# Where the two operands of a matmul lie in on-chip memory: stationary parts moved to a fixed distance from the moving ones, and the feed-forward's high parts put ahead of its low ones

## The chip, the cores and the metric

The kernel runs on one core of a Trainium2 chip. The metric is device time in microseconds (us) of one launch, the median over runs. TensorE (PE in the profile) multiplies; VectorE (DVE), ScalarE (ACT) and GpSimd (POOL) work on tiles in on-chip memory; SyncE (SP) issues most of the transfers from the chip's main memory.

## What is computed

One layer of a decoder on 256 tokens of 1,024 features, float32 throughout:

```python
h = rms_norm(x);  x = x + hybrid_mixer(h)          # conv module and sparse attention, one projection
h = rms_norm(x);  x = x + cross_attention(h, mem)  # 4 heads of 256, 256 memory tokens
h = rms_norm(x);  x = x + swiglu(h)                # D_FF = 2816
return rms_norm(x, final_norm_g)

def swiglu(h, w_in, w_out):
    a, b = jnp.split(h @ w_in, 2, axis=-1)
    return (jax.nn.silu(a) * b) @ w_out
```

`hybrid_mixer` projects `h` to conv inputs, queries, keys, values and gates; runs a causal 31-tap convolution with a layer norm, and attention over compressed, selected and window keys; gates both, and projects once more.

## The kernel before

**Products in three passes.** A float32 product is made of matmuls of the type fp32r. Each operand is split into a high part, a rounded copy made on ACT (line 179 for weights, 290 for activations), and a low part, the difference, made on DVE (lines 181 and 291). A product is then high × high, high × low and low × high, added up in PSUM. Some projections (`whole`, line 267: k0, kc, vc, q) use plain float32 matmuls without a split.

**The gemms.** The activations are held transposed, feature by token, as tiles of 8 × 256 elements in each of the 128 partitions. A weight block `name` is 1,024 × 256, loaded in two halves of 512 × 256 (`raw`, line 205), each split into two tiles (`split`, line 172). `gemm` (line 257) runs both halves through `rows` (line 235): three passes of 2 × 4 matmuls, 24 per half and 48 per block, each with a stationary operand of 128 × 128 (`lhsT`, loaded by a separate instruction that PE overlaps with the matmul before) and a moving operand (`rhs`) of 128 × 256. Mostly the weights are stationary and the activations move; for vs, vw and v (`nat=True`) the activations are stationary and the weights move.

**Where the tiles lie.** Tiles are given out by tag in the order in which the code first asks for them. The long tiles of 8,192 bytes per partition (tags `L0` to `L14`) and the double one `LL` of 16,384 come first and begin at byte 4,608 = 9 × 512, so all of them lie at 0 modulo 512, and so does every slice of 128 or 256 elements of them. The activations' parts lie in them. Then come five buffers `wh` and five `wl` for the high and low parts of weights. Each is 1,048 elements, 4,192 bytes, so from one buffer to the next the start moves by 96 modulo 512; `at` (line 173) shifts each group of five splits by another 16 bytes. High and low part of one half have the same offset (the buffers of `wl` begin at 480, and the low part 32 bytes into them). So the halves of u0 to u7 lie at 400, 304, 112, 208, 32, 416, 320, 128, 224, 48, 432, 336, 144, 240, 64 and 448; v0's first half at 448; xq1's second half at 64; f8's first half and f20's second at 0; f7's first half at 288. The transposed query tiles of cross-attention (tag `vt`) lie at 0 or 256.

**The order around the change.** Instructions run on each engine in the order that the scheduler gives them from the code; `behind(...)` holds an instruction until a marked one has been issued before it on the same engine, and `in_line()` does that for PE's own sequence. In the attention part (lines 813 to 880) the 8 head pairs go one after the other: `scores` for the next pair (PE, then DVE with line 735 for the first 128 tokens and 741 for the others), `weights` (ACT's exp, line 756), some rows of gc and v gemms from `between`, then `turned` (PE transposes, line 777, and ACT copies, line 780, listed in `copies`). The softmax over compressed blocks, `compressed_weights` (lines 692 to 704), is one set of instructions on the tile `nsc`; it is called in the first period ahead of that period's `weights`, and its result is transposed at line 857 in the third. `first[...]` names instructions behind which a given split is held. The convolution's taps run on POOL (lines 424 and 428), ACT (426) and DVE (412) beside the gemms of the first 180 us.

**The feed-forward** (lines 1046 to 1065) loops over 22 blocks j of `ffn_in_w`, each with 128 columns of a (b = 0) and 128 of b (b = 1). The moving operand of the high pass is `fg[:, :, kb]`, high and low part of the activations side by side, 512 columns; the low pass moves 256. Per j the order is: b = 0 high (8 matmuls), b = 0 low (8), b = 1 high, b = 1 low. Even j use the PSUM banks of `mm`, odd j those of `s`, two each. The result u is split into three pairs of long tiles. At the end (lines 1075 to 1083) u's parts are stationary and the weights `fo` move, 512 columns, 264 matmuls.

Of the kernel before, what the change touches and what calls it, by code (L numbers as in the profile page):

```python
# [15 lines left out]
P = 128  # L16
# [82 lines left out]
def tile_hybrid_block(  # L99
# [26 lines left out]
    def longs(names, slots, dt=F32R):  # L126
        return [long(n, i, dt=dt) for n, i in zip(names, slots)]

    def twin(name, dt=F32R):

        t = sb.tile([P, 2, NB, S], dt, tag="LL", name=name)
        return t, t[:, 0], t[:, 1]

    def small(name, shape, dt=F32, tag=None, bufs=1):
# [26 lines left out]
    def roots(at):  # L161

        return nc.scalar.activation(table[:, at:at + 1], eps_t[:, 0:1], AF.Sqrt)
# [6 lines left out]


    def split(w, shape, name):
        at = 4 * (len(splits) // 5 % 5)
        hi, lo = (small(f"{name}{c}", [P, 1024 + 24], F32R, tag=f"w{c}", bufs=5)[:, n:n + 1024].rearrange("p (k c) -> p k c", k=shape[1])
                  for c, n in (("h", at), ("l", at + 8)))

        n = 2 if name == "k1_0" else shape[1]
        with behind(*first.get(name, ())):
            copies = [nc.scalar.activation(hi[:, at:at + n], w[:, at:at + n], AF.Copy) for at in range(0, shape[1], n)]  # L179
            for at in range(0, shape[1], n):  # L180
                low = nc.vector.tensor_tensor(out=lo[:, at:at + n], in0=w[:, at:at + n], in1=f(hi[:, at:at + n]), op=ALU.subtract)  # L181
        splits[name] = copies[-1], low
        return hi, lo
# [13 lines left out]
    def ahead(name, slot, pieces=(4, 4)):  # L197
# [3 lines left out]
        for n in pieces:  # L201
            nc.sync.dma_start(w[:, at:at + n], wst[CHUNK_AT[name]][:, at:at + n])
            at += n

    def raw(name, i):

        if name in held:
            return held[name][:, 4 * i:4 * i + 4]
        w = small(f"{name}_{i}", [P, 4, 256], tag="w", bufs=4)
        loads[f"{name}_{i}"] = nc.sync.dma_start(w, wst[CHUNK_AT[name]][:, 4 * i:4 * i + 4])  # L210
        return w

# [146 lines left out]
    for name, slot in (("k2", 12), ("k3", 11), ("u0", 13)):  # L359
        ahead(name, slot)  # L360
    roots(0)

    def kx(j):
        ps = gemm(f"k{j}", mem) if j else whole("k0", mem_t)
# [327 lines left out]
    def compressed_weights(*marks):  # L692

        mc = small("mc", [P, 2, HEADS])
        with behind(*marks):
            nc.vector.tensor_reduce(out=mc, in_=nsc, axis=AX.X, op=ALU.min)
        with behind(*marks, mins_of[1]):
            nc.vector.tensor_tensor(out=nsc, in0=nsc, in1=mc.unsqueeze(3).to_broadcast([P, 2, HEADS, 16]), op=ALU.subtract)
            nc.scalar.activation(nsc, nsc, AF.Exp, scale=-1.0)
            nc.vector.tensor_reduce(out=sumc, in_=nsc, axis=AX.X, op=ALU.add)  # L700
            nc.vector.scalar_tensor_tensor(out=sumc, in0=sumc, scalar=1e-30, in1=igc, op0=ALU.max, op1=ALU.mult)
            nc.vector.reciprocal(sumc, sumc)
            nc.vector.tensor_tensor(out=sumc, in0=sumc, in1=cpt[:, CP_CM:CP_CM + 2].unsqueeze(2).to_broadcast([P, 2, HEADS]), op=ALU.mult)
            nc.vector.tensor_tensor(out=nsc, in0=nsc, in1=sumc.unsqueeze(3).to_broadcast([P, 2, HEADS, 16]), op=ALU.mult)
# [5 lines left out]
    def scores(hp):  # L710

        g = hp // 2
        nbp = bias_of(hp)
        s0 = aux(f"s0_{hp}", [P, 2, 2, P], "s0", 1)
        p0 = small(f"p0_{hp}", [P, 2, 2, P], tag="p0", bufs=2)
        s1s, p1 = [], []

        def later_half(hd):
            s1 = aux(f"s1_{hd}", [P, 2, S], "s", 2)
            with in_line():  # L720
                for i, t in enumerate((kdh, kdl)):
                    mm = nc.tensor.matmul(s1, lhsT=qh(hd, 1), rhs=t[:, g].rearrange("p b t -> p (b t)"), start=i == 0, stop=i == 1)
            last[:] = [mm]
            s1s.append(s1)

        later_half(2 * hp)
        for k, hd in enumerate(heads_of(hp)):
            with in_line():
                for i, t in enumerate((kdh, kdl)):
                    mm = nc.tensor.matmul(s0[:, k], lhsT=qh(hd, 0), rhs=t[:, g, :, 0:P], start=i == 0, stop=i == 1)  # L730
        last[:] = [mm]
        later_half(2 * hp + 1)
        for k, hd in enumerate(heads_of(hp)):
            for br in range(2):
                red = nc.vector.tensor_tensor_reduce(out=p0[:, k, br], in0=s0[:, k, br], in1=nbp[:, k, P:S], scale=1.0, scalar=3e38,  # L735
                                                     op0=ALU.add, op1=ALU.min, accum_out=mins[:, hd, 0, br:br + 1])
        for k, hd in enumerate(heads_of(hp)):
            p1.append(small(f"p1_{hd}", [P, 2, S], tag="pr", bufs=4))
            for br in range(2):
                with behind(red):  # L740
                    low = nc.vector.tensor_tensor_reduce(out=p1[k][:, br], in0=s1s[k][:, br], in1=nbp[:, k], scale=1.0, scalar=3e38,
                                                   op0=ALU.add, op1=ALU.min, accum_out=mins[:, hd, 1, br:br + 1])
        mins_of.append(low)
        if hp == 1:
            first["gc2_1"] = first["gc3_0"] = red,
        return p0, p1

    def weights(hp, p0, p1, *late):
# [96 lines left out]
    for hp, n in enumerate(PERIODS):  # L845
        if hp < 7:
            p.append(scores(hp + 1))
            if hp == 0:
                compressed_weights(*exp[-2:])
            with behind(*copies[-3:]):  # L850
                weights(hp + 1, *p[hp + 1])
        if hp == 2:
            pc_ps = aux("pc_ps", [P, 4, P], "pt", 2)
            with in_line():
                for qb in range(2):
                    for i in range(2):
                        mm = nc.tensor.transpose(pc_ps[:, 2 * i + qb], nsc[:, qb, 8 * i:8 * i + 8].rearrange("p h n -> p (h n)"), ident)
            last[:] = [mm]
            nc.scalar.activation(pct.rearrange("p i q -> p (i q)"), pc_ps.rearrange("p i q -> p (i q)"), AF.Copy)

        with behind(*last):
            if hp == 3:
                total = rnorm(total, "l")
            elif hp == 5:
                layer_norm_scale(total)
        rest(n - AFTER)
        if len(turns) == 2:
            output(hp // 2 - 1, turns)
            turns = []
        p0, p1 = p[hp]  # L870
        tb = turned(f"b{hp}", [p1[k][:, br, P:S] for k in range(2) for br in range(2)])
        ta = [turned(f"a{hd}", [q for br in range(2) for q in (p0[:, k, br], p1[k][:, br, 0:P])])
              for k, hd in enumerate(heads_of(hp))]
        turns.append((ta, tb))
        if hp == 1:
            with behind(*last, *copies[-3:]):
                total = layer_norm_squares(total)
        rest(AFTER)
# [36 lines left out]
    def residual(products, xin, gain, name, slots):  # L915

        xo = long(f"x_{name}", slots[0])
        g, gh, gl = twin(f"g_{name}") if len(slots) == 1 else (None, *longs((f"gh_{name}", f"gl_{name}"), slots[1:]))
        acc = small(f"acc_{name}", [P, S], tag="vw", bufs=4)
        for j, (n, ps) in enumerate(products):  # L920
            js = slice(2 * j, 2 * j + 2)
# [25 lines left out]

    def cross_queries(j):
        ps = gemm(f"xq{j}", xg)
        queries[j] = [small(f"xq{c}{j}", [P, 2, S], F32R, tag="vt", bufs=4) for c in "hl"]  # L950
        part(queries[j][0][:], queries[j][1][:], ps[:])

    def cross_scores(j):
# [75 lines left out]

    rf = small("rf", [P, S], tag="vw", bufs=4)  # L1030
    nc.scalar.activation(rf, spread(rnorm(acc2, "3"), "3"), AF.Copy)
    uh, ul = (longs([f"u{c}{i}" for i in range(3)], ss) for c, ss in (("h", (4, 2, 1)), ("l", (5, 3, 6))))
    def residual_first():

        banks = [[aux(f"fo{c}_{tb}", [P, 512], t, n) for tb, (t, n) in enumerate(ts)]
# [10 lines left out]
    for j in range(NF):  # L1046
        hs = chunk(f"f{j}")
        ab = small(f"ab{j}", [P, 2, S], tag="pr", bufs=4)
        for b in range(2):

            ps = bank(f"ps_f{j}_{b}") if j % 2 == 0 else aux(f"ps_f{j}_{b}", [P, 2, S], "s", 2)
            cs = slice(b * P, b * P + P)
            for kb in range(NB):
                nc.tensor.matmul(ps, lhsT=hs[kb // 4][0][:, kb % 4, cs], rhs=fg[:, :, kb], start=kb == 0, stop=False)  # L1054
            for kb in range(NB):
                nc.tensor.matmul(ps[:, 1], lhsT=hs[kb // 4][1][:, kb % 4, cs], rhs=fg[:, 0, kb], start=False, stop=kb == NB - 1)  # L1056
            nc.scalar.activation(ab[:, b], ps[:, 0], AF.Copy)  # L1057
            nc.vector.tensor_tensor(out=ab[:, b], in0=ps[:, 1], in1=ab[:, b], op=ALU.add)  # L1058
        nc.vector.tensor_tensor(out=ab, in0=ab, in1=rf.unsqueeze(1).to_broadcast([P, 2, S]), op=ALU.mult)
        sl = small(f"sl{j}", [P, S], tag="sg", bufs=3)  # L1060
        silu = nc.scalar.activation(sl, ab[:, 0], AF.Silu)  # L1061
        nc.vector.tensor_tensor(out=sl, in0=sl, in1=ab[:, 1], op=ALU.mult)
        part(uh[j // 8][:, j % 8], ul[j // 8][:, j % 8], sl[:])
        if j == 2:
            accs = residual_first()

# [8 lines left out]
    def to_output(c, tb, his, los):  # L1075

        ts = slice(tb * P, tb * P + P)
        for k0, hi in his.items():
            for k in range(2):
                kb = k0 + k  # L1080
                th, tl = (u[kb // 8][:, kb % 8, ts] for u in (uh, ul))
                for t, w in ((th, hi), (th, los[k0]), (tl, hi)):
                    nc.tensor.matmul(accs[c][tb], lhsT=t, rhs=w[:, k], start=False, stop=kb == NF - 1 and t is tl)  # L1083

# [158 lines left out]
```

## Time and profile before

| | |
|---|---|
| median of 3 runs | 561.68 us (561.3 to 562.07) |
| the profiled execution | 562.13 us |
| its span, first to last instruction | 560.3 us |
| mean granted clock of PE | 0.997 |
| PE busy | 551.0 us |
| PE's weight loads busy | 508.0 us |
| DVE, ACT, POOL busy | 415.4, 362.5, 146.3 us |
| read from main memory | 95.39 MB |

PE's matmuls overlap: one lasts about 280 ns at 256 columns, but the next starts well before it ends. So the rate is read from starts, not from durations. A row of the view of instructions in order of time has the start, the time that the row's instructions cover, the engine, the line, the operation, what it writes and reads, and the count; a row of the chain has start, time, and what. L246 is line 246 of the kernel.

### The profile page before, as it was taken

The numbers are of one execution on the slowest core, as the hardware profiler recorded it, in microseconds if no ns is written. First come the engines' busy times: TensorE is split into PE (matmuls) and PEld (weight loads), VectorE is DVE, ScalarE is ACT, GpSimd is POOL, SyncE is SP. The second block draws the span as 40 slices with busy tenths as digits, with TensorE's granted clock in tenths as the row PEclk, the third lists the DMA queues.
The fourth block names the chain that finished last, engine by engine and source line by source line (L and its number), as shares of the span: only waits on it lengthen the run. The fifth ranks groups of instructions, "written<-read, shape, count | busy, mean of one in ns | idle before, by whom it ended". The sixth has DMA issues, their size and how long they took to land.

```text
span 560.3 us, 10256 instructions
## 1 busy us (share of the span) xinstructions
PE 551.0 (98%) x3886; PEld 508.0 (91%) x3886; DVE 415.4 (74%) x772; ACT 362.5 (65%) x689; POOL 146.3 (26%) x129
## 2 busy tenths in 40 slices
PE   8999999999999999999999999999999999999995
PEld 7999998889999999999999999988888888888883
DVE  2798985898978999794768666578878787864531
ACT  3577757689957898789546565567565656563421
POOL 0005997989999102000003100230000000000000
PEclk9999999999999999999999999999999999999998
DMA  8938714356365554334554542446555555666601
GB/s 297 412 108 307 301 45 121 113 187 217 128 204 171 180 187 138 99 113 151 176 192 160 185 156 76 150 151 225 181 196 183 192 181 196 183 198 189 189 32 75
DMA packets 29298, 97.31 MB, mean 174 GB/s; under 512 B 3136, under 2 KB 5952, under 8 KB 28992
## 3 DMA queue, kind: packets, MB, share of 16 engines
q1 hardware_dynamic: 28528, 95.34, 51.4%
q10 hardware_dynamic: 720, 1.31, 0.7%
q8 instruction: 30, 0.49, 0.4%
q14 instruction: 20, 0.16, 0.1%
HBM read 95.39 MB, written 1.25 MB: 172 GB/s over the span
## 4 chain that ended last, share of the span: by engine, by line
PE 82%; POOL 7%; ACT 3%; DVE 2%; DMA 2%; issue 2%; ACTq 0%; POOLq 0%
PE ps_f L1054 15%; PE fo L1083 11%; PE ps_u L246 8%; PE ps_f L1056 7%; POOL yt L428 6%; PE ps_pw L246 4%; PE ps_v L246 4%; PE ps_wo L246 4%; PE ps_xq L246 4%; PE ps_k L246 3%; PE ps_q L276 3%; PE ps_xo L246 3%; PE ps_gc L246 2%; DMA mem_t<-in_memt_dram 2%; PE ps_xo L1021 2%
## 5 line engine op out<-in xcount | busy, mean ns | idle before, releaser
L428 POOL TENSOR_TENSOR yt<-yt,vw 128x512 f32<-128x512 f32 x65 | 100.9, 1553 | 56.5 <-ACT vw L426 52.7
L426 ACT ACTIVATE vw<-vt,ppt 128x256 f32<-128x256 f32 x110 | 48.0, 499 | 14.8 <-POOL yt L428 14.6
L1054 PE MATMUL ps_f<-g,f_1h 128*128 128x512 f32 x176 | 48.6, 396 | 0.0
L1054 PE MATMUL ps_f<-g,f_0h 128*128 128x512 f32 x176 | 48.2, 396 | 0.0
L1125 POOL TENSOR_SCALAR x<-x,rr 128x512 f32<-128x512 f32 x1 | 0.7, 693 | 179.8 <-DVE rr L1095 179.8
L181 DVE TENSOR_TENSOR f_1l<-f,f_1h 128x1024 fp32r<-128x1024 f32 x22 | 26.9, 1224 | 22.5 <-ACT sl L1061 18.3
L412 DVE SCALAR_TENSOR_TENSOR yp<-vt,ppt,yp 128x256 f32<-128x256 f32 x100 | 40.9, 482 | 0.1
L1054 PEld LDWEIGHTS ps_f<-g,f_1h 128*128 128x128 f32 x176 | 32.8, 188 | 7.5
L756 ACT ACTIVATE p<-p,mins 128x128 f32<-128x128 f32 (+1 forms) x64 | 28.2, 443 | 10.0 <-DVE mins L735 10.0
L1054 PEld LDWEIGHTS ps_f<-g,f_0h 128*128 128x128 f32 x176 | 30.0, 188 | 4.0
L1057 ACT ACTIVATE ab<-ps_f 128x256 f32<-128x256 f32 x44 | 16.5, 374 | 25.8 <-PE ps_f L1056 25.8
L1056 PEld LDWEIGHTS ps_f<-g,f_0l 128*128 128x128 f32 x176 | 26.9, 188 | 3.7
L179 ACT ACTIVATE f_1h<-f 128x1024 fp32r<-128x1024 f32 x22 | 23.3, 1058 | 8.5 <-PE ps_f L1054 8.3
L276 PE MATMUL ps_q<-hf,q 128*128 128x256 f32 x128 | 28.5, 381 | 0.0
L1056 PE MATMUL ps_f<-g,f_1l 128*128 128x256 f32 x176 | 28.2, 281 | 0.0
L1056 PE MATMUL ps_f<-g,f_0l 128*128 128x256 f32 x176 | 28.0, 281 | 0.0
L181 DVE TENSOR_TENSOR f_0l<-f,f_0h 128x1024 fp32r<-128x1024 f32 x22 | 27.4, 1244 | 0.0
L276 PEld LDWEIGHTS ps_q<-hf,q 128*128 128x128 f32 x128 | 24.1, 190 | 3.3
L179 ACT ACTIVATE f_0h<-f 128x1024 fp32r<-128x1024 f32 x22 | 23.1, 1049 | 5.3 <-PE ps_xo L1021 4.7
L1056 PEld LDWEIGHTS ps_f<-g,f_1l 128*128 128x128 f32 x176 | 23.9, 188 | 0.0
L931 POOL COPY acc<-s_wo 128x256 f32<-128x256 f32 x1 | 0.7, 660 | 71.6 <-ACT s_wo L924 71.6
L1058 DVE TENSOR_TENSOR ab<-ps_f,ab 128x256 f32<-128x256 f32 x44 | 18.4, 420 | 0.7 <-ACT ab L1057 0.6
(543 smaller groups left out, 1564.4 us busy)
## 6 DMA issues: line engine op xcount, KB each, us to landing
f<-in_wst_dram SPq DMA_DIRECT2D x44, 512.0 KB, 3.7
fo<-in_wfo_dram SPq DMA_DIRECT2D x22, 512.0 KB, 4.3
u<-in_wst_dram SPq DMA_DIRECT2D x14, 512.0 KB, 6.1
q<-in_wst_dram SPq DMA_DIRECT2D x8, 512.0 KB, 4.9
ga<-in_wst_dram SPq DMA_DIRECT2D x8, 512.0 KB, 3.7
gc<-in_wst_dram SPq DMA_DIRECT2D x8, 512.0 KB, 3.8
v<-in_wst_dram SPq DMA_DIRECT2D x8, 512.0 KB, 4.5
pw<-in_wst_dram SPq DMA_DIRECT2D x8, 512.0 KB, 4.4
```

Of the source, the lines that this page charges most:

```text
L179: copies = [nc.scalar.activation(hi[:, at:at + n], w[:, at:at + n], AF.Copy) for at in range(0, shape[1], n)]
L181: low = nc.vector.tensor_tensor(out=lo[:, at:at + n], in0=w[:, at:at + n], in1=f(hi[:, at:at + n]), op=ALU.subtract)
L246: mm = nc.tensor.matmul(ps[:, b], lhsT=lhsT, rhs=rhs, start=row + b + kb == 0, stop=kb == NB - 1 and row == 2 and b == 1)
L276: mm = nc.tensor.matmul(ps[:, b], lhsT=w[:, k, cs], rhs=x[:, kb], start=kb + b == 0, stop=kb == NB - 1 and b == 1)
L412: nc.vector.scalar_tensor_tensor(out=out[:, i] if t == ts[-1] else acc[i], in0=v, scalar=w, in1=acc[i], op0=ALU.mult, op1=ALU.add)
L426: nc.scalar.activation(pr[:, i], v, AF.Identity, scale=w, bias=col(PP_DB, j + i) if t == 0 else 0.0)
L428: nc.gpsimd.tensor_tensor(out=y, in0=y, in1=pr, op=ALU.add)
L756: exp.append(nc.scalar.activation(t, t, AF.Exp, scale=-1.0, bias=mins[:, hd, qb, br:br + 1], accum_out=sums[:, hd, qb, br:br + 1]))
L1054: nc.tensor.matmul(ps, lhsT=hs[kb // 4][0][:, kb % 4, cs], rhs=fg[:, :, kb], start=kb == 0, stop=False)
L1056: nc.tensor.matmul(ps[:, 1], lhsT=hs[kb // 4][1][:, kb % 4, cs], rhs=fg[:, 0, kb], start=False, stop=kb == NB - 1)
L1058: nc.vector.tensor_tensor(out=ab[:, b], in0=ps[:, 1], in1=ab[:, b], op=ALU.add)
L1083: nc.tensor.matmul(accs[c][tb], lhsT=t, rhs=w[:, k], start=False, stop=kb == NF - 1 and t is tl)
```

## The change

1. The buffers of split weights become 1,024 elements, 4,096 bytes, without the shift `at`. A new tile of 16 elements, 64 bytes, is given out ahead of them, so they lie at 64 modulo 512.
2. The tags are now `whi` (five buffers), `wlo` (five) and `w` (four, the raw halves, as before). `w` is given out later, behind two small tiles of 32 bytes each and others of multiples of 128, and lies at 128. For the feed-forward's input weights `w` and `wlo` change roles: the raw halves go to `wlo`, the low parts to `w`.
3. The moving parts of the feed-forward, `fg`, begin 64 bytes into their double tile; u's parts, now in four pairs of long tiles of 6 × 256, 64 bytes into theirs; the query parts of cross-attention 192 bytes into theirs.
4. In the feed-forward the order per j is b = 0 high, b = 1 high, b = 0 low, b = 1 low, and both evacuations follow.
5. `compressed_weights` is called after the first period's `turned`, its exp on ACT is held behind the first of the copies, and the split of gc3's first half is held behind that copy and the second pair's last reduction instead of the second pair's L735.

```diff
-    def twin(name, dt=F32R):
-        t = sb.tile([P, 2, NB, S], dt, tag="LL", name=name)
+    def twin(name, dt=F32R, at=0):
+        t = sb.tile([P, 2 * NB * S + 128], dt, tag="LL", name=name)[:, at:at + 2 * NB * S].rearrange("p (c k s) -> p c k s", c=2, k=NB)
...
     def split(w, shape, name):
-        at = 4 * (len(splits) // 5 % 5)
-        hi, lo = (small(f"{name}{c}", [P, 1024 + 24], F32R, tag=f"w{c}", bufs=5)[:, n:n + 1024].rearrange("p (k c) -> p k c", k=shape[1])
-                  for c, n in (("h", at), ("l", at + 8)))
+        hi = small(f"{name}h", shape, F32R, tag="whi", bufs=5)
+        lo = small(f"{name}l", shape, F32R, **places[1 - into_ffn(name)])
...
+    places = dict(tag="w", bufs=4), dict(tag="wlo", bufs=5)
+    def into_ffn(name):
+        return name[0] == "f" and name[1] != "o"
...
-        w = small(f"{name}_{i}", [P, 4, 256], tag="w", bufs=4)
+        w = small(f"{name}_{i}", [P, 4, 256], **places[into_ffn(name)])
...
     roots(0)
+    small("gap", [P, 16])
...
-            nc.scalar.activation(nsc, nsc, AF.Exp, scale=-1.0)
+            with behind(copies[0]):
+                nc.scalar.activation(nsc, nsc, AF.Exp, scale=-1.0)
...
-            first["gc2_1"] = first["gc3_0"] = red,
+            first["gc2_1"] = red,
...
-            if hp == 0:
-                compressed_weights(*exp[-2:])
...
         turns.append((ta, tb))
+        if hp == 0:
+            compressed_weights(*exp[-2:])
+            first["gc3_0"] = copies[0], mins_of[1]
...
-        g, gh, gl = twin(f"g_{name}") if len(slots) == 1 else ...
+        g, gh, gl = twin(f"g_{name}", at=16) if len(slots) == 1 else ...
...
-        queries[j] = [small(f"xq{c}{j}", [P, 2, S], F32R, tag="vt", bufs=4) for c in "hl"]
+        queries[j] = [small(f"xq{c}{j}", [P, 2 * S + 48], F32R, tag="vt", bufs=4)[:, 48:].rearrange("p (d s) -> p d s", d=2) for c in "hl"]
...
-    uh, ul = (longs([f"u{c}{i}" for i in range(3)], ss) for c, ss in (("h", (4, 2, 1)), ("l", (5, 3, 6))))
+    uh, ul = ([long(f"u{c}{i}", n, (P, 6 * S + 16), F32R)[:, 16:].rearrange("p (k s) -> p k s", k=6) for i, n in enumerate(ss)]
+              for c, ss in (("h", (4, 2, 1, 12)), ("l", (5, 3, 6, 13))))
...
-        for b in range(2):
-            ps = bank(f"ps_f{j}_{b}") if j % 2 == 0 else aux(f"ps_f{j}_{b}", [P, 2, S], "s", 2)
-            cs = slice(b * P, b * P + P)
-            for kb in range(NB):
-                nc.tensor.matmul(ps, lhsT=hs[kb // 4][0][:, kb % 4, cs], rhs=fg[:, :, kb], start=kb == 0, stop=False)
-            for kb in range(NB):
-                nc.tensor.matmul(ps[:, 1], lhsT=hs[kb // 4][1][:, kb % 4, cs], rhs=fg[:, 0, kb], start=False, stop=kb == NB - 1)
+        pss = [bank(f"ps_f{j}_{b}") if j % 2 == 0 else aux(f"ps_f{j}_{b}", [P, 2, S], "s", 2) for b in range(2)]
+        for part_ in range(2):
+            for b, ps in enumerate(pss):
+                cs = slice(b * P, b * P + P)
+                for kb in range(NB):
+                    w = hs[kb // 4][part_][:, kb % 4, cs]
+                    if part_:
+                        nc.tensor.matmul(ps[:, 1], lhsT=w, rhs=fg[:, 0, kb], start=False, stop=kb == NB - 1)
+                    else:
+                        nc.tensor.matmul(ps, lhsT=w, rhs=fg[:, :, kb], start=kb == 0, stop=False)
+        for b, ps in enumerate(pss):
             nc.scalar.activation(ab[:, b], ps[:, 0], AF.Copy)
...
-        part(uh[j // 8][:, j % 8], ul[j // 8][:, j % 8], sl[:])
+        part(uh[j // 6][:, j % 6], ul[j // 6][:, j % 6], sl[:])
```

More of the change, by code (lines that the diff above doesn't have):

```diff
@@ L917, in residual @@
         xo = long(f"x_{name}", slots[0])
-        g, gh, gl = twin(f"g_{name}") if len(slots) == 1 else (None, *longs((f"gh_{name}", f"gl_{name}"), slots[1:]))
+        g, gh, gl = twin(f"g_{name}", at=16) if len(slots) == 1 else (None, *longs((f"gh_{name}", f"gl_{name}"), slots[1:]))
         acc = small(f"acc_{name}", [P, S], tag="vw", bufs=4)
@@ L1080, in to_output @@
                 kb = k0 + k
-                th, tl = (u[kb // 8][:, kb % 8, ts] for u in (uh, ul))
+                th, tl = (u[kb // 6][:, kb % 6, ts] for u in (uh, ul))
                 for t, w in ((th, hi), (th, los[k0]), (tl, hi)):
```

## The prediction

> **What bounds the kernel now.** I read the page's head first, then who PE waited for, then the chain that ended last in order of time, then PE's own instructions in order of time.
>
> ```profile
> span 560.3 us, 10256 instructions
> PE 551.0 (98%) x3886; PEld 508.0 (91%) x3886; DVE 415.4 (74%) x772; ACT 362.5 (65%) x689; POOL 146.3 (26%) x129
> ...
> PE ps_k L276 <- DMA mem_t<-in_memt_dram: 1.0, 2, 0.5
> PE s L730 <- ACT ptt_b L780: 0.5, 1, 0.5
> ...
> 34.00:79.00 45.00, 45.00 (x381) 44.73 (x380) 40.92 (x68) 30.40 (x57) 29.27 (x22) 1.00 0.66 232
> ...
> 383.00:492.30 109.30, 109.30 (x627) 95.56 (x626) 83.90 (x138) 66.41 (x119) 0.00 (x0) 1.00 0.58 189
> ```
>
> PE is busy in 98% of the span, and after the start it waits once, for 0.5 us. The last two lines are stretches, the u gemms and the feed-forward: PE busy throughout at clock 1.00, in the second DVE for 83.90 of 109.30 us and ACT for 66.41, DMA at 0.58. So the time is the number of matmuls times the step from one start to the next. The chain gives that step:
>
> ```profile
> 34.40 43.98 PE ps_u L246 x374
> ...
> 261.57 22.96 PE ps_pw L246 x192
> 284.54 17.06 PE ps_wo L246 x144
> ...
> 360.78 5.61 PE ps_xo L246 x48
> ...
> 394.27 1.86 PE ps_f L1054 x8
> 396.14 0.95 PE ps_f L1056 x8
> ...
> 492.36 61.29 PE fo L1083 x264
> ```
>
> The columns are start, time and count. The first four rows, matmuls of 256 moving columns, are 758 in 89.61 us, 118.2 ns each. The feed-forward's high parts, 512 columns, take 1.86/8 = 232.5 ns, its low parts, 256 columns, 118 ns, the output matmuls, 512 columns, 61.29/264 = 232.2 ns. No semaphore ends anything inside these rows, so a change of the step is a change of the span.
>
> **Does the step follow the addresses?** In the kernel before, every half block of weights lies at another offset modulo 512, while the moving activations of these gemms lie at 0, so the trace holds the experiment already. Here are PE's rows of u6's first half (stationary at 144) and second (240), of both halves of u7 (64 and 448), then of u3's first half (320) and xq1's second half (64):
>
> ```profile
> 67.09 1.11 PE L246 MATMUL ps_u<-hh,u_0h 128*128 128x256 f32 x8
> ...
> 69.96 1.10 PE L246 MATMUL ps_u<-hh,u_1h 128*128 128x256 f32 x8
> ...
> 72.77 1.07 PE L246 MATMUL ps_u<-hh,u_0h 128*128 128x256 f32 x8
> ...
> 75.49 1.07 PE L246 MATMUL ps_u<-hh,u_1h 128*128 128x256 f32 x8
> ...
> 78.21 0.81 PE L468 MATMUL rel_ps<-tables 128*128 128x384 f32 x2
> ...
> 50.08 1.11 PE L246 MATMUL ps_u<-hh,u_0h 128*128 128x256 f32 x8
> ...
> 52.91 0.27 PE L246 MATMUL ps_u<-hh,u_1h 128*128 128x256 f32 x1
> ...
> 316.13 1.07 PE L246 MATMUL ps_xq<-gh,xq_1h 128*128 128x256 f32 x8
> 317.03 1.07 PE L246 MATMUL ps_xq<-gl,xq_1h 128*128 128x256 f32 x8
> ```
>
> From start to start of a half are 24 matmuls. At 144: 2.87 us, 119.6 ns. At 240: 2.81, 117.1. At 64: 2.72, 113.3. At 448, right behind it: 2.72, 113.3. At 320: 2.83, 117.9. In xq1 at 64 the eight take 0.90 us, 112.5 at this rounding. So 64 above has a step some 5 ns shorter than the usual one, in two places with different data. The clock is not it: 1.00 in the stretch of u that holds both. One pair speaks against a plain rule: v0's first half has its weights as the moving part at 448 and its activations as the stationary part at 0, also 64 above modulo 512, and takes the slow step, 0.94/8 = 117.5 ns:
>
> ```profile
> 215.87 1.10 PE L246 MATMUL ps_v<-v_0h,memh 128*128 128x256 f32 x8
> 216.81 1.11 PE L246 MATMUL ps_v<-v_0h,meml 128*128 128x256 f32 x8
> ```
>
> So I read 64 as the offset at which the short step can settle, and mostly does, not as one that forces it.
>
> The Trainium skill, "SBUF — State Buffer", section "Who interferes with whom", says that PE reads the moving operand and the weights through two independent ports and never waits on anyone. By that rule the offsets are worth nothing and the sum below would keep only its edits of order; the trace disagrees, 113.3 against 119.6 ns in one run of u.
>
> **The change part by part.** No matmul, copy or transfer is added or removed; what is changed is where tiles lie and the order. The profiled execution takes 562.13 us, 0.45 above the median 561.68 of the runs shown; I work out the difference and take it from the median.
>
> *Weights stationary, 256 columns.* k1 to k3, u, ks, kw, ga, gc, pw, wo, xq, xo: 37 blocks of 48, 1,776 matmuls. By the diff all parts ahead of the new 64-byte tile stay at multiples of 512, and both kinds of split buffer follow at 64, each 4,096 bytes. So all 37 blocks stand where u7's first half stood. I take 114.0 rather than 113.3, because gc and xq are cut by other matmuls and have to settle again: 1,776 × 4.2 = 7.5 us. Ends: all at 113.3, 8.7; half of them slow at 117.9, so 115.95 in the mean, 4.0.
>
> *Weights moving, 256 columns.* vs, vw, v: 6 × 48 = 288. There the activations, stationary, stay at 0 and the weights move at 64: 64 below. No row shows that pair; the nearest are u7's second half (64 below, 113.3) and v0 (117.5). I take 116.5: 288 × 1.7 = 0.5, ends 0.2 and 1.4.
>
> *Feed-forward low parts.* 352 matmuls, stationary at 128 over moving parts at 64. They come in runs of 16 behind a 512-column matmul. Between 113.3 and 117.7 I take the middle, 115.5, for 118: 352 × 2.5 = 0.9, ends 0.1 and 1.7.
>
> *512 columns.* 352 high parts and 264 output matmuls, at difference 0. Two half blocks of before stand at difference 0, f8's first and f20's second; with them the slowest four that I find, f7's first half at 288:
>
> ```profile
> 413.71 1.09 PE L1054 MATMUL ps_f<-g,f_0h 128*128 128x512 f32 x4
> 414.64 1.09 PE L1054 MATMUL ps_f<-g,f_1h 128*128 128x512 f32 x4
> ...
> 481.93 1.07 PE L1054 MATMUL ps_f<-g,f_1h 128*128 128x512 f32 x4
> 482.84 0.63 PE L1056 MATMUL ps_f<-g,f_0l 128*128 128x256 f32 x4
> ...
> 408.12 1.10 PE L1054 MATMUL ps_f<-g,f_0h 128*128 128x512 f32 x4
> 409.06 1.09 PE L1054 MATMUL ps_f<-g,f_1h 128*128 128x512 f32 x4
> ```
>
> 0.93/4 = 232.5 and 0.91/4 = 227.5 at difference 0, 0.94/4 = 235.0 at worst. I take 230.6, a little above the middle of the first two: the mean of before is 232.4, so 616 × 1.8 = 1.1; ends 3.0 and −0.1.
>
> *High parts of both blocks first.* Per j 16 high and 16 low as before. Two banks are open at once and a high buffer is freed earlier, a low one later; both evacuations come after the low parts. They hide under the next j: DVE's 83.90 of 109.30 us is 4.3 us of 5.6 per j. Without that cover one j would cost a copy and an addition once, under 1 us. Worth 0, ±0.5.
>
> *The compressed softmax moved.* Its exp on ACT (L699) goes behind the first transposed copy, and its minimum on DVE (L696) behind the next scores:
>
> ```profile
> 186.94 0.68 DVE L696 TENSOR_REDUCE mc<-nsc 128x32 f32<-128x512 f32 x1
> ...
> 192.34 0.62 ACT L699 ACTIVATE nsc<-nsc 128x512 f32<-128x512 f32 x1
> 192.86 0.57 ACT L780 ACTIVATE ptt_b<-pt_b 128x512 f32<-128x512 f32 x1
> ...
> 192.54 0.40 PE L722 MATMUL s<-kdl,qt 128*128 128x512 f32 x1
> 193.49 0.38 PE L730 MATMUL s<-kdh,qt 128*128 128x256 f32 x1 [0.55 <-ACT ptt_b L780]
> ...
> 201.27 0.68 DVE L704 TENSOR_TENSOR nsc<-nsc,sumc 128x512 f32<-128x512 f32 x1
> ...
> 204.30 0.60 PE L857 MATMUL pc_ps<-cpt,nsc 128*128 128x128 f32 x4
> ```
>
> PE's one real stall is here: 0.95 us from start to start where 0.23 is usual, 0.7 lost. The exp stands 0.52 us ahead of the copy that PE waits for, so the move returns 0.5 to 0.7. What is queued behind the waiting exp on ACT are v's first split and the next exps; who needs the result is L857, at 204.30, 2.3 us after L704 ends. A delay of about 1 us fits in. But PE arrives earlier: from 113 us the chain runs over POOL and ACT, not PE, and ks, kw, ga and half of gc, 384 matmuls, save 384 × 4.2 = 1.6 us under it:
>
> ```profile
> 113.69 1.29 POOL yt L428
> ...
> 158.07 2.16 POOL yt L428
> ...
> 110.00:160.00 50.00, 50.00 (x368) 47.27 (x366) 44.78 (x65) 41.63 (x82) 47.36 (x33) 1.00 0.54 182
> ```
>
> The first two rows are the first and the last of POOL's run in the chain, the third the stretch: POOL is busy in 47.36 of 50.00 us. If that chain does not move at all, the stall grows to 0.7 + 1.6 − 0.6 = 1.7; if it moves with PE it is gone. I book the middle, 0.8, which is 0.1 us worse than before.
>
> *Sum:* 7.5 + 0.5 + 0.9 + 1.1 − 0.1 = 9.9 us. 561.68 − 9.9 = 551.8.
>
> **The rivals.** *Half of the runs settle slow, and the POOL chain keeps what PE saves* (for it: v0; against it: u7 and xq1): 4.0 + 0.2 + 0.1 − 0.1 − 1.0 = 3.2 less, 558.5; half way to the forecast it is 555.2. *Slower: the two streams lock on the long step everywhere.* One mechanism, in every gemm: 256 columns at 117.7 and 512 columns at 235.0, which long runs at one difference would repeat 616 times. 2,064 × 0.5 = 1.0 and 352 × 0.3 = 0.1 less, 616 × 2.6 = 1.6 and the stall 1.0 more: 563.2. It decides once the 512-column step is above 234.2 with the others at 117.7 (616 × 1.8 = 1.1), sooner if the stall grows. For it: f7, v0; against: f20. *Addresses do nothing, or the tiles don't lie as I count them:* then only the stall's half microsecond is left, 561.2. Against it speak 113.3 and 119.6 ns in one gemm; for it, that a buffer may come to lie elsewhere than I count. The rule of the skill's page above is this case.
>
> **How the numbers follow.** Forecast 0.60, the partial gain 0.25, slower 0.06, nothing 0.09. The range reaches down to all terms at their good ends, 8.7 + 1.4 + 1.7 + 3.0 + 0.7 = 15.5 less, 546.2, of which I leave a little out, and up past the partial case: 546.5 to 559.0. A difference of 0.2% (1.1 us) is about what a measurement of this kernel can tell from none: faster by over that 0.86, within 0.08, slower 0.06.
>
> **What would show it.** In PE's rows in order of time: 24 matmuls of u, pw, wo in 2.72 us each half, in all halves alike; v's halves at 2.72 or 2.83; eight high parts of the feed-forward in 1.84, sixteen low in 1.85; the output row at 60.9 or less for 264. ACT's ptt_b copy ahead of the exp, and the gap before L730 below or near 0.95. I am wrong if u's halves still differ from one another, if 64 gives 2.83 us, or if PE's waits grow beyond 2 us.

## The result, and the profile after

The changed kernel takes 557.03 us in the median of five runs (555.37 to 558.62), the kernel before 561.93 beside it; the ratio is 0.9916 with an interval of 0.9888 to 0.9943. So 4.9 us are gained where 9.9 were forecast. That is between the partial rival, 558.5, and half way from it to the forecast, 555.2. The partial rival, which had been given a chance of 0.25, is 1.5 us off, the forecast 5.2. The runs also lie wider apart, 3.25 us against 0.83. The profiled execution is the longest of the five, 558.62 us.

The head of the page, then the waits of PE (microseconds in total, times, longest):

```profile
span 556.8 us, 10220 instructions
...
PE 543.9 (98%) x3886; PEld 501.9 (90%) x3886; DVE 415.2 (75%) x772; ACT 362.8 (65%) x689; POOL 144.9 (26%) x129
```
```profile
PE ps_k L280 <- DMA mem_t<-in_memt_dram: 2.3, 2, 1.9
...
PE s L737 <- ACT ptt_b L787: 1.0, 1, 1.0
PE pt_b L784 <- DVE mins L742: 0.8, 1, 0.8
PE fo L1095 <- DVE fo_4l L180: 0.5, 1, 0.5
PE ps_f L1067 <- DVE ab L1070: 0.3, 1, 0.3
```

PE is 7.1 us less busy, but the span is only 3.5 shorter. 1.5 of the 7.1 us lie ahead of the first split gemm, k1, where a longer wait for the tile `mem_t`, 2.3 us for 1.0, takes the place of busy time; k1 begins no later (14.29 us for 14.46). After the start, waits of 1.0, 0.8, 0.5 and 0.3 us have come in where there was one of 0.5. The chain that ended last (start, time, what, count):

```profile
34.11 44.05 PE ps_u L250 x374
...
261.36 21.97 PE ps_pw L250 x192
283.33 16.32 PE ps_wo L250 x144
...
299.88 5.44 PE ps_wo L250 x48
305.32 5.44 PE ps_xq L250 x48
...
357.80 5.65 PE ps_xo L250 x48
...
383.97 3.65 PE ps_f L1067 x16
387.62 1.89 PE ps_f L1065 x16
...
495.75 54.30 PE fo L1095 x238
```

The rows of u, pw and wo are the result. (A step is the time from one matmul's start to the next one's; a difference is where the stationary operand lies less where the moving one lies, modulo 512 bytes.) pw and wo, 336 matmuls, took 22.96 + 17.06 = 40.02 us, 119.1 ns a step, and take 21.97 + 16.32 = 38.29, 114.0 with the entry's few long steps in it. u, 374 matmuls, took 43.98 and takes 44.05: 117.8 ns a step, although its operands stand at the same difference of 64 as those of pw and wo. In the feed-forward sixteen high parts take 3.65 us, 228 ns each, where they took 232.5; sixteen low ones 1.89 us, 118 ns as before.

### The profile page after: what moved, and what is told of

Same layout as the page of the kernel before. It is cut to its first block, busy times and chain, and to the rows that moved or that the text cites. A ratio compares the mean times of both kernels' runs of the same rounds, so it can differ in the third digit from the quotient of the medians.

```text
span 556.8 us, 10220 instructions
## 1 busy us (share of the span) xinstructions
PE 543.9 (98%) x3886; PEld 501.9 (90%) x3886; DVE 415.2 (75%) x772; ACT 362.8 (65%) x689; POOL 144.9 (26%) x129
## 4 chain that ended last, share of the span: by engine, by line
PE 78%; POOL 8%; DVE 4%; issue 3%; DMA 3%; ACT 3%; ACTq 0%; POOLq 0%; DVEq 0%
PE ps_f L1067 14%; PE fo L1095 10%; PE ps_u L250 8%; POOL yt L434 7%; PE ps_f L1065 7%; PE ps_v L250 4%; PE ps_xq L250 4%; PE ps_pw L250 4%; PE ps_wo L250 4%; PE ps_k L250 3%; PE ps_q L280 3%; PE ps_xo L250 3%; DMA mem_t<-in_memt_dram 2%; PE ps_xo L1029 2%; DMA fo<-in_wfo_dram 1%
## 5 line engine op out<-in xcount | busy, mean ns | idle before, releaser
L1067 PEld LDWEIGHTS ps_f<-g,f_0h 128*128 128x128 f32 x176 | 31.5, 189 | 5.8 <-DVE ab L1070 0.5
L1065 PEld LDWEIGHTS ps_f<-g,f_0l 128*128 128x128 f32 x176 | 25.5, 188 | 1.8
L1070 DVE TENSOR_TENSOR ab<-ps_f,ab 128x256 f32<-128x256 f32 x44 | 16.8, 416 | 0.6 <-ACT ab L1069 0.6
```

The source lines that it names most:

```text
L1065: nc.tensor.matmul(ps[:, 1], lhsT=w, rhs=fg[:, 0, kb], start=False, stop=kb == NB - 1)
L1067: nc.tensor.matmul(ps, lhsT=w, rhs=fg[:, :, kb], start=kb == 0, stop=False)
```

## What the theories say

**Theory A.** At a difference of 64 the 256-column step has two stable values, 113.3 and 117.8 ns. A run of matmuls takes one of them when it begins behind a break (plain float32 matmuls, transposes, 512 columns, a wait) and keeps it until the next break; the first steps behind a break are its entry. **Rival B.** The value belongs to the place: what DVE, POOL or the transfers do beside u and not beside pw. **Rival C.** Offsets do nothing, and the gain is the order's.

## The experiments

**again, again2, again3: the changed kernel unchanged**, run three times more.

> The changed kernel unchanged, for a second profile. Theory A (at difference 64 the 256-column step has two stable values, 113.3 and 117.8 ns, and which one a run of matmuls keeps is settled anew at each entry, differently from one execution to the next): k1 to k3 and u, at 117.8 in the first profile, need not be slow again, and pw, wo and xq0, at 113.3, need not be fast again; the shares change by some hundreds of matmuls, and the span by 1 to 3 us from 556.8. Rival B (the slow places are slow because of what else runs there: POOL, DVE or DMA traffic): the same blocks are slow and fast as in the first profile, all of u at 117.8, pw and wo at 113.3, and the span is within 0.5 us of 556.8.

> The changed kernel once more, on the chip of the two others. Theory A: a median near 557 with executions spread over some 3 us, and in the profile u wholly at 113.3 or wholly at 117.8 ns, or changing at one of its breaks, with pw at 113.3 and ga3 at 117.8 as in both profiles so far.

> The changed kernel beside best on the same chip: 557 within half a microsecond, executions spread over 3 us; in the profile u at 113.3 or 117.8 ns and pw at 113.3, as in the three profiles so far.

Measured: 554.95 us for the first (one execution), medians of 557.46 (556.13 to 558.80) and 557.70 (554.90 to 558.37) for the others. The chain of again:

```profile
33.27 42.39 PE ps_u L250 x374
...
122.86 5.65 PE ps_ks L250 x48
128.52 5.66 PE ps_kw L250 x48
...
258.79 21.97 PE ps_pw L250 x192
```

The same program, the same addresses: u in 42.39 us instead of 44.05, 113.3 ns; and ks and kw in 5.65 and 5.66 for 48, 117.8. In the first profile these were at 113.3, as PE's rows of ks show, eight matmuls from 127.94 to 128.84 us and eight more to 129.75:

```profile
127.94 1.07 PE L250 MATMUL ps_ks<-hh,ks_1h 128*128 128x256 f32 x8
128.84 1.07 PE L250 MATMUL ps_ks<-hl,ks_1h 128*128 128x256 f32 x8
129.75 1.07 PE L250 MATMUL ps_ks<-hh,ks_1l 128*128 128x256 f32 x8
```

In the profile of again 445 steps in a row, from the second half of k2 to the end of u, hold 113.3. again2 and again3 have u in 44.05 again. pw takes 21.97 in all four profiles, and the blocks ga3, gc0 and xo3 are at 117.8 in all four. Rival B falls: the place does not set the value, since u and ks changed theirs. In each of the four profiles the split gemms make 47 unbroken runs on PE, and no run goes from one value to the other once it has held one for four steps. 40 of the 47 have the same value in all four; the seven that change are k1, the run from k2 to u, the one from ks to vw, and four in gc. The profiles of again, again2 and again3 come from three chips, but on one chip again3's six executions still spread over 3.5 us, those of the kernel before beside them over 0.8.

**zero: all gemms at difference 0.**

```diff
-    small("gap", [P, 16])
-        g, gh, gl = twin(f"g_{name}", at=16) if ...
+        g, gh, gl = twin(f"g_{name}") if ...
```
(and the query parts and u's parts back to the beginning of their tiles)

> The changed kernel with the 64-byte gap taken out and the moving parts back at 0: all 256-column gemms at difference 0 modulo 512, the feed-forward's high and output matmuls at 0 as in the changed kernel, its low parts 64 above as there; order edits kept. Theory A: difference 0 has no fast value, u in a long run takes about 120 ns; 2,064 matmuls at 120 instead of about 116 cost some 8 us, so 564 to 566, slower than before. Theory C (offsets do nothing, the gain comes from the order): 557, as the changed kernel.

Measured: 563.67 us, 1.0033 of before (1.0022 to 1.0044).

```profile
33.78 44.88 PE ps_u L250 x374
...
262.77 23.22 PE ps_pw L250 x192
```

120.0 ns in every long run, 23.22 us for pw against 21.97. The order edits are in this kernel too, so the gain of the changed kernel is the offsets'. Rival C falls.

**addr_only, order_only, comp_only: the edits apart.** addr_only has the offsets with the old order of the feed-forward and the old place of the compressed softmax; order_only is the kernel before with both edits of order; comp_only the kernel before with the compressed softmax moved alone.

> The changed kernel with the offsets alone: the feed-forward's order per j and the compressed softmax's place are those of before. Theory A: the order edits cost about 2 us in the profile of the changed kernel (1.0 at the start of the feed-forward, 1.2 between 193 and 261 us), so without them 554 to 556; the feed-forward's step of 512 columns is unsettled in runs of 8 and not 16, which gives back up to 1 us. Theory C: 561 to 562, the gain is gone.

> The kernel before with the two order edits alone (both blocks' high parts first; the compressed softmax moved), offsets as before. Theory A: no gain, 561 to 563; the start of the feed-forward 1 us later than before and the stall of 192.5 us 0.5 shorter. Theory C: 557 as the changed kernel.

> The kernel before with the compressed softmax moved and nothing else. Both order edits together gave 0.7 us. If it is this move: 561.1, and no stall of 0.7 us ahead of the scores at 192 us. If it is the feed-forward's order: 561.8.

Measured: 557.10 us (0.9904, 0.9886 to 0.9922); 561.14 (0.9988, 0.9979 to 0.9996); 561.37 (0.9992, 0.9983 to 1.0001). The offsets alone are worth what the whole change is. The cost of 2 us that theory A had put on the order edits isn't there: with the offsets alone PE waits as long (1.0 us for ptt_b, 0.8 for the minimum), and the feed-forward from its first matmul to block 3 takes 20.19 us with the old order against 20.43 with the new. With the new order it takes 19.30 in again and 19.38 in order_only, as in the kernel before, 19.38: this start varies from one execution to the next, whatever the order. Past it, a block takes 5.56 us in addr_only and 5.54 in the changed kernel, so both high parts first is worth some 0.4 us over 22 blocks, less than the start varies. The move of the compressed softmax shifts the stall and doesn't end it: in order_only and comp_only PE no longer waits at 193 us, but 0.66 and 0.73 us for the next pair's ptt_b, at 203.62 and 202.56.

The 0.7 us of order_only are real by their interval. Its profile has every stage from k1 to the last matmul as long as before within 0.1 us; from the last matmul's start to the end of the span it takes 6.4 us against 7.1, and comp_only's does too. This end is 6.1 to 6.4 us in five profiles, with and without the offsets (addr_only, kick, best, order_only, comp_only), and 7.1 to 7.2 in all others. That it is this end which makes the 0.7 us between the medians is not shown.

**low320, low192: the feed-forward's low parts at another difference**, 320 or 192 instead of 64, by a tile of 256 or 128 bytes ahead of the tag `w` (and the rest of 512 behind it).

```diff
+        if not into_ffn(name) and "pw" not in first:
+            first["pw"] = small("pad_w", [P, 64])      # 32 for low192
         w = small(f"{name}_{i}", [P, 4, 256], **places[into_ffn(name)])
```

> The changed kernel with the feed-forward's low parts 256 bytes further up, so their stationary part lies 320 above the moving one and not 64. In the changed kernel all 16 of a block j take 117.8 ns each, because a run of 512 columns locked at 226.5 stands ahead of them. Theory A1 (what an entry settles on depends on where the weights lie against the stream that runs, so another difference can enter fast): 113.3, 22 x 16 x 4.5 = 1.6 us less in the feed-forward, 5.47 us per j instead of 5.55. Theory A2 (out of the locked 512 columns the entry is always slow): 117.8 and 5.55 as before.

> As low320, with the low parts 192 above the moving ones. A1: 113.3 and 5.47 us per j, or, if 192 has no short step, 118 and 5.55. A2: 117.8 and 5.55.

Measured: 558.48 and 558.44 us (one execution each), u in 44.05 in both. The chain of low320:

```profile
389.16 3.65 PE ps_f L1071 x16
392.81 1.89 PE ps_f L1069 x16
```

The low parts stay at 118, as by A2 of the expectation: behind 512 columns that run at 226.5, none of the three differences 64, 192 and 320 gives them the short step (from the third block on; the first two are cut by waits and other matmuls). low192 takes 3.69 for the high parts besides.

**hi64: the feed-forward wholly at 64.**

```diff
+            first["pw"] = small("pad_w", [P, 112])
...
-        g, gh, gl = twin(f"g_{name}", at=16) if ...
+        g, gh, gl = twin(f"g_{name}") if ...
```

> The changed kernel with the feed-forward's activations 64 bytes lower and its low parts 64 bytes lower too: the low parts keep their difference of 64, the high parts, 512 columns, stand 64 above instead of 0. If 512 columns need the difference 0 for their 226.5 ns: 232 again, 16 x 5.5 x 22 = 1.1 us to 1.9 us more in the feed-forward, 5.60 to 5.63 us per j. If 64 has the short step for them as well: 5.55.

Measured: 555.84 us (one execution, with u in 42.39). Its chain:

```profile
386.46 3.73 PE ps_f L1071 x16
390.19 1.82 PE ps_f L1069 x16
```

At 64 the 512 columns are at 233 ns again, 0.08 us more for sixteen. But behind them the low parts take the short step, 1.82, 0.07 less. A block takes 5.55 us, where 5.60 to 5.63 were expected, and 5.54 with the high parts at 0. Out of high parts at 226.5 the low parts begin with the long step, out of high parts at 233 with the short one; no run here has both gains together.

**wlo224: an entry for every half block.** The low parts of all weights but the feed-forward's at 224, by tiles ahead of and behind the tag `wlo`.

```diff
+        if "pl" not in first:
+            first["pl"] = small("pad_l", [P, 40])
         lo = small(f"{name}l", shape, F32R, **places[1 - into_ffn(name)])
+        if "pm" not in first:
+            first["pm"] = small("pad_m", [P, 88])
```

> The changed kernel with the low parts of all other weights at 224 modulo 512 instead of 64, the high parts at 64 as they are; the last 8 matmuls of each half of 24 then stand at a difference that has no lasting step in the kernel before (224 there: 116 to 120 ns in turn), and each half enters 64 anew. Theory A (a run keeps the value of its entry): the lottery of long runs ends; if the entry out of 224 is fast, as the one out of 240 into u7 was, each half takes (16 x 113.3 + 8 x 118) / 24 = 114.9 ns in all gemms, those slow in both profiles included (ga3, gc0, xq1, xo3), and runs differ by under 1 us; the output matmuls with low weights lose their 0 difference and take 232 instead of 226.5, 88 x 5.5 = 0.5 us more: 555 to 556. If the entry is slow: 117.9 everywhere, 560 to 561. Rival B (the place sets the step): pw and wo at 113.3 in the 16, ga3 and gc0 at 117.8 as in both profiles.

Measured: 557.34 us (0.9932, 0.9911 to 0.9953).

```profile
33.41 42.81 PE ps_u L254 x374
...
259.41 22.26 PE ps_pw L254 x192
```

u is at 42.81 / 374 = 114.5 ns (114.9 was expected), and ga3, gc0 and xo3, at 117.8 in all four profiles of the changed kernel, are at 114.4 to 114.6: the 16 high matmuls of a half at 113.3, the 8 low ones at 116.7. So the entry decides, and one out of 224 goes to the short step with stationary weights: of those that run on for six matmuls or more 60 of 61 do, here and in the profile of best, and the one that doesn't, in xq at 316 us, has three low matmuls in a row ahead of it instead of eight. Where the weights move (vs, vw, v), the difference is 288 and the same entry went to 117.9 six times of seven. The gain is paid at the output matmuls: their low weights leave difference 0, and not only these 88 get slower, as expected, but all 264, to a mean of 232.5 ns without the waits against 227.3. So the time missed the 555 to 556 expected, and the four executions lie 2.4 us apart (556.81 to 559.19) where under 1 was expected. What still varies there is open.

**kick, kick3: an entry only where a break stands.** The low parts of the first half of 17 blocks (kick), or of both halves of k3 and the first of xq1 (kick3), change places with their raw halves, as the feed-forward's do, and so lie at 128.

```diff
+    kicks = {f"{n}_0" for n in "k3 ks ga3 gc1 gc2 gc3 v0 v1 v2 v3 xq1 xq2 xq3 xo0 xo1 xo2 xo3".split()}
+    def swapped(name):
+        return into_ffn(name) or name in kicks
```

> The changed kernel, with the low parts of the first half of 17 blocks (k3, ks, ga3, gc1 to gc3, v0 to v3, xq1 to xq3, xo0 to xo3), which stand behind a break, moved to the buffers at 128 modulo 512; 8 matmuls of each such block then run at a difference with no lasting step, and what follows enters 64 anew. All else, the output matmuls too, as in the changed kernel. Theory A: if the entry out of 128 is fast, as the one out of 224 was, u takes 113.3 ns in each execution, and so do ga3's second half, gc0, the later xq and xo: gemms in about 200.5 us of steps instead of 202.5, 554 to 555, with executions within 1 us of one another. If that entry is slow, u stays at 117.8 always: 558 to 559. Rival B: ga3, gc0, xo3 at 117.8 as before, and the spread stays at 3 us.

> As kick, with three half blocks alone in the other buffers: both halves of k3, ahead of u, and xq1's first. Theory A: two entries out of 128 ahead of u leave it slow in few executions, 384 x 4.5 = 1.7 us less in those that had it slow; xq1's second half and xq2 gain some 60 x 4.5 = 0.3 us; and without kick's late weights at 187 us nothing is lost: 555.5 to 556.5, profile with u at 113.3. If an entry out of 128 is again a lottery, u is slow in some executions still and the spread of 3 us stays.

Measured: 560.52 us (0.9982, 0.9973 to 0.9991) and 558.16 (0.9934, 0.9921 to 0.9948; runs 1.3 us apart). In both profiles u is at 113.3, but k3 was so already ahead of its low parts at 128, so this proves nothing. In kick the steps went from 117.8 to 113.3 behind the first halves of ga3 and xq1, and stayed at 117.8 behind that of ks: out of 128 the short step is not sure. And the exchange of buffers delays the weights. kick's PE, in order of time, and the stretch behind its wait (us, busy time of PE, PEld, DVE, ACT and POOL, granted clock, share of the DMA engines, GB/s):

```profile
189.41 1.09 PE L789 MATMUL pt_b<-cpt,p 128*128 128x128 f32 x4 [3.33 <-DVE mins L747]
...
191.85 2.06 PE L255 MATMUL ps_gc<-hl,gc_1h 128*128 128x256 f32 x8
```
```profile
191.85:195.50 3.65, 3.65 (x19) 3.64 (x18) 3.58 (x13) 3.35 (x8) 0.00 (x0) 0.55 0.74 238
```

ACT's copy of gc's next half waits 3.5 us for its transfer, DVE's split for the copy, the minima queue behind the split, and PE stands still for 3.33 us. Its clock, granted in full until 188 us, is half from some 188.3 to 195 us, and the gc matmuls follow one another every 213 ns. What this half clock costs beside the wait is not shown: DVE is busy for 3.58 of those 3.65 us, and three of kick's eleven executions, with a mean clock of 0.996 to 0.997 instead of 0.992 or 0.993, take 559.7 to 561.1 us all the same. kick3 has a wait of 1.5 us in the cross-attention. Neither gains as much as was expected, 554 to 555 and 555.5 to 556.5.

**best: wlo224 without its price.** Low parts at 224; for the output weights too the low parts and the raw halves change places; `w` lies at 64, the feed-forward's activations at 0.

```diff
-    def into_ffn(name):
-        return name[0] == "f" and name[1] != "o"
+    def swapped(name):
+        return name[0] == "f"
...
-        w = small(name, list(src.shape), tag="w", bufs=4)
+        w = small(name, list(src.shape), **places[swapped(name)])
```
(with wlo224's tiles, 160 bytes ahead of `wlo`, 288 behind it and 64 behind `w`; the feed-forward's parts as in hi64; the query parts 256 bytes into their tiles)

> The changed kernel with wlo224's offset of the low parts, and its cost at the output matmuls taken back: their low parts use the other buffers, which lie at 64 like the high parts, so all 264 stand at difference 0; the feed-forward's activations are 64 bytes lower, as in hi64, so its parts stand at 64. Theory A: wlo224's 557.3 less 1.2 us for the output matmuls, 555.8 to 556.5; gemms with stationary weights at 114.4 in each execution, and less spread than the changed kernel. If the entry out of 224 is a lottery too, 557 as the changed kernel.

Measured: 554.69 us (554.43 to 555.12), 0.9875 of before (0.9862 to 0.9888); the changed kernel beside it, again3, 557.70, 0.9917 (0.9900 to 0.9935). That is 1.1 us below what was expected. The intervals don't meet, and the runs of best lie within 0.7 us, those of again3 within 3.5.

```profile
33.56 42.81 PE ps_u L256 x374
...
170.00 5.50 PE ps_ga L256 x48
...
259.59 22.26 PE ps_pw L256 x192
...
387.19 3.74 PE ps_f L1073 x16
390.93 1.82 PE ps_f L1071 x16
...
487.04 59.87 PE fo L1101 x264
```

The entry out of 224 holds in a second kernel, ga3 included, and the output takes 59.87 us, 226.7 ns each without a wait. 1.0 us of this profile's lead lies behind the last matmul (6.1 us from its start to the end of the span, 7.1 before), in transfers that no edit touches. addr_only and kick have this short end too, without best's offsets, so it is not best's own; how much of the 3.0 us between the medians of best and again3 is owed to it is open.

## Why the prediction was wrong

Each stage from its first matmul to the next stage's, from PE's rows in order of time: the forecast's terms sorted by stage, and what four profiles of the changed kernel and the one of best gained on the profile before, all in us.

| stage, its time before | forecast | first profile | again | again2 | again3 | best |
|---|---|---|---|---|---|---|
| k1 to ks (k, u), 110.8 | 528 x 4.2 = 2.2 | 0.0 | 2.2 | 0.0 | 0.0 | 1.6 |
| ks to pw (ks to v), 136.3 | 480 x 4.2 + 0.5 - 0.1 = 2.4 | 0.0 | 0.1 | 0.0 | 0.1 | 0.0 |
| pw to the feed-forward, 104.7 | 768 x 4.2 = 3.2 | 2.7 | 2.7 | 2.7 | 2.7 | 2.8 |
| feed-forward, 126.0 | 0.9 + 352 x 1.8 = 1.5 | 0.2 | 1.3 | 1.0 | 0.5 | 0.5 |
| output, 61.0 | 264 x 1.8 = 0.5 | 0.5 | 0.4 | 0.3 | 0.6 | 1.4 |

*The step that failed: "I take 114.0 rather than 113.3" for all 37 blocks.* Over the steps that no break interrupts, the mean of these blocks was 118.15 ns before and is 116.0 in the first profile, 114.9 in again, 115.9 in the two others. Over 1,776 matmuls that is 3.8, 5.8 and 4.0 us where 7.5 were booked, and what the stages that hold them gained is 2.7 to 2.9 us in three of the profiles and 5.0 in again (the first three rows of the table). The reading of before was right as far as it went (u7 and xq1 at 113.3, and v0 at 117.5 as the pair that spoke against it), and the text drew the right sentence from it: 64 is an offset at which the short step can settle. But the sum then priced it as if it settled wherever a run is long, and left only short runs slower. What settles is the entry, and a long run makes it worse: u, 374 matmuls, is lost as a whole or won as a whole. "24 matmuls in 2.72 us each half" was the sign named for right, 2.83 the one for wrong; u has 2.83 in every half in the first profile, 2.72 in again. The bound of half the runs slow, 4.0 us, was the better guess of the size, and it was put only at the end of the term and into the rival. That 557.03 lies within 546.5 to 559.0 is owed to the room left for that rival, not to the sum.

*"I book the middle, 0.8"* for what the attention's chain keeps. It keeps everything, so "a change of the step is a change of the span" does not hold here. From ks to pw is 136.28 us before and 136.28 after, 136.2 to 136.3 in again, again2, again3 and best, whatever the steps inside are between 113 and 118 ns (zero, at 120, takes 137.2): in the first profile the unbroken steps of gemms and v are 1.7 us shorter in all, and as much is lost at waits and around them. Here are the two, PE's rows, then ACT's around them:

```profile
188.45 0.63 PE L784 MATMUL pt_b<-cpt,p 128*128 128x128 f32 x4 [0.83 <-DVE mins L742]
...
203.26 0.39 PE L737 MATMUL s<-kdh,qt 128*128 128x256 f32 x1 [1.02 <-ACT ptt_b L787]
```
```profile
191.51 0.57 ACT L787 ACTIVATE ptt_b<-pt_b 128x512 f32<-128x512 f32 x1
191.98 0.62 ACT L706 ACTIVATE nsc<-nsc 128x512 f32<-128x512 f32 x1
...
201.69 1.04 ACT L178 ACTIVATE v_0h<-v 128x1024 fp32r<-128x1024 f32 x1
202.64 0.57 ACT L787 ACTIVATE ptt_b<-pt_b 128x512 f32<-128x512 f32 x1
```

The copy does stand ahead of the exp now, as forecast, and the stall ahead of 193.49 us is gone. But the next pair's copy queues behind v's split at 201.69, and PE waits 1.02 us for it; and 0.83 for a minimum on DVE that before came in time. POOL's chain, which the prediction named, is not what keeps the time in each profile: in again the chain that ended last has no POOL work in this stage and runs over ACT and DVE from 188.3 to 200.7 us, and the stage is 136.2 us all the same. The prediction named the danger and its size (1.7 us) and then took the middle, with nothing to say why the chain should give half.

*"Between 113.3 and 117.7 I take the middle, 115.5"* for the low parts: 117.8, no gain of the 0.9. The middle of two stable values is a value that no run settled at.

*512 columns* did better than the 230.6 taken: 228.7 for the high parts (230.1 for the first eight of a block, which settle, 226.5 for the other eight) and 227 for the output. The output gave back most of its 1.4 us at waits for split weights (0.52 at fo_4), which best, with other buffers, hasn't: there it is the 1.4. *Both high parts first*, taken as 0 ± 0.5, is worth the 0.4 us above. That the addresses count stands: 120.0 ns at 0, 113.3 or 117.8 at 64. The Trainium skill, "SBUF — State Buffer", section "Who interferes with whom", gives PE two independent ports; by it zero would have taken 557, and it took 563.67.

What sends an entry one way or the other isn't settled. The runs show that it depends on what runs ahead (out of eight matmuls at 224 short with stationary weights, out of 512 columns at 226.5 long at the three differences tried) and that for seven of the 47 runs, k1, k2 and ks among them, it changes between executions. That these stand behind waits for transfers or other engines, whose length varies, is only argued.

## What to carry to other kernels

Where a trace shows a short and a long step for the same instruction, find out how a run came into its step before pricing it: where two values are stable, their mean, and not the better one, belongs into the sum, run by run and not matmul by matmul. A repeated profile of the same program separates what changes by chance (seven runs here) from what comes out the same each time (40). A gain under a stretch that other engines end (136.3 us here with any step from 113 to 118 ns) is to be booked at zero until that stretch itself gets shorter.

## What the runs showed of the hardware

The step of a 256-column fp32r matmul depends on where its two operands lie modulo 512 bytes: 120.0 ns at 0 (zero), 113.3 or 117.8 at 64 and held for some 445 steps (u and the blocks ahead of it), 113 to 120 in turn at 224 (wlo224, best), 113 to 124 at 128 (kick); 512 columns take 226.5 at 0 and 233 at 64 (hi64). That the modulus is 512, and not a divisor of it such as 256, no run shows. In kick PE's last matmul ahead of its wait of 3.33 us ended at 186.1 us; its granted clock was 0.66 on average from 188 to 189 us and 0.50 from there to 195, and the 256-column step was 213 ns. The Trainium skill, "TensorE: Matmul & The Clock Gate", Part 1, says that an idle window of about 3.4 us brings the clock to half; this trace agrees on the half, but shows it some 2.2 us after the last matmul.
